# Moving blocks and up weights at other byte offsets in a two-layer encoder kernel

## The chip, the core and the metric

The kernel runs on one core of a Trainium2 chip. The metric is the time on the device in microseconds, taken over repeated runs of the program. The profile is that of one execution, recorded by the hardware profiler. Engines are called as the profile calls them: PE is the matrix engine (TensorE), PEld its weight loads, DVE VectorE, ACT ScalarE, POOL GpSimd, SP SyncE.

## What is computed

Two encoder layers on 256 tokens of width 2048. Each has a token mixer (neighbourhood attention in the first layer, grouped-query attention in the second), run together with cross-attention into 256 memory tokens and one output projection, and then a feed-forward block of width 8192. The change touches the feed-forward block alone:

```python
for i in range(DEPTH):
    ...
    h = h + jnp.concatenate([mix, cross], axis=-1) @ w_o[i]
    n = rms_norm(h, mlp_norm[i])
    h = h + jnp.square(jax.nn.relu(n @ w_up[i])) @ w_down[i]
return rms_norm(h, final_norm)
```

All weights and activations are float32.

## The kernel before

**Two halves for every operand.** TensorE multiplies a shorter float format, so each float32 operand is split into a high and a low part: `split` (L297 to L300) has ScalarE copy the source into the high tile (the write rounds) and VectorE write source minus high into the low tile. A product is then three matmuls: high by high, high by low, low by high.

**The feed-forward block.** The 8192 inner features are cut into 8 parts of 1024. The *up* product of a part (`up_grains`, `u_products`) takes the weights as the stationary operand, 128 by 128 at a time from the tiles `uh` and `ul`, and the activations `hT` as the moving operand, 256 columns. One grain is a half tile of 1024 elements, 24 matmuls; 16 grains make a part, 384 matmuls. `squared` takes the result out, squares it, and makes the stationary tiles `a` of the *down* product.

The down product of the first seven parts (`down_grains`) is one level of Strassen's scheme with seven block products instead of eight. Here the activations `a` are stationary, and the blocks made from the weights are moving, 512 columns at a time: the first group (`FIRST`, three products) from `bh` and `bl` (three blocks each), the second (`SECOND`, four products) from `th` and `tl` (four blocks each). Before the split VectorE and an accumulating transfer on POOL's queue add up the blocks of `t` from those of `b` (L758, L759, L767, L768). One pair of grains is 9 + 12 = 21 matmuls; a part has eight such pairs. The eighth part has no partner and goes through `plain_grains`, with `uh`, `ul`, `th`, `tl` as moving tiles (its matmuls stand at L205, L208 and L209, in the helper `m_products`, which the projections use too, with the moving tiles `hi` and `lo`).

**Order.** `add_mlp` writes the order out by hand: the up grains of part 0 alone, and then, for each of the 56 pairs, up grain, first group, up grain, second group, where the up grains are those of the part after. `run_all` prepares grains some places ahead (`SOON`), so that loads and splits run beside the matmuls. The framework's scheduler then orders the instructions of each engine; in the trace the 48 up matmuls of a pair of grains mostly stand together, followed by the 21 of the pair product. The text calls these 69 a step.

**Where tiles lie.** `bh`, `bl`, `th`, `tl`, `z`, `c` and `a` are in the pool `mlp`, one behind the other from the left of the memory; `bh`, `bl`, `th`, `tl` exist once each. `uh`, `ul` (two buffers each), the loaded weights `U`, `b`, `T` and the scratch tile `junk` are in the pool `side`, which ends at the right. Every tile starts at a multiple of 32 bytes in its partition. `th`, `tl`, `bh`, `bl`, `a`, `hi`, `lo`, `cat` and `memT` start 128 bytes after a multiple of 256; `hT` and `nT`, which share one place, 160 after; `uh`, `ul` and the rest of `side` 224 after. All slices that a matmul reads begin a multiple of 512 bytes into a tile. The memory is nearly full: 1,376 bytes are free between the two sides during the feed-forward block.

**The junk tile.** `sum_squares` (L584) has ScalarE square 512 columns of `h` and keep the sum of each row; the squares themselves go to `junk`, which nothing reads.

Of the kernel before, what the change touches and what calls it, by code (L numbers as in the profile page):

```python
# [11 lines left out]
F32R = mybir.dt.float32r  # L12
BF16 = mybir.dt.bfloat16
# [4 lines left out]
P = 128  # L18
# [15 lines left out]
CH = 2048  # L34
HALF = CH // 2
GROUP = 2
PARTS = 8
PK = DFF // PARTS // P
STEPS = PK // 2
GUARD = 3  # L40
# [30 lines left out]
def encoder_kernel(ctx: ExitStack, tc: tile.TileContext, t: dict, out: bass.AP):  # L71
# [225 lines left out]
    def split(dst_hi, dst_lo, src):  # L297

        nc.scalar.activation(dst_hi, src, AF.Copy)  # L299
        nc.vector.tensor_tensor(dst_lo, src, dst_hi.bitcast(F32), op=ALU.subtract)  # L300
# [281 lines left out]


    def sum_squares(which, i, nb):  # L584
        sq = at.side.tile([P, 512], BF16, tag="junk", bufs=2, name="sq")
        nc.scalar.activation(sq, h[:, i, nb * 512 : (nb + 1) * 512], AF.Square,
                             accum_out=ssq[which][:, i, nb : nb + 1])

# [82 lines left out]
            nc.tensor.matmul(ps, hi[:, s], acts[:, k, SEQ:], start=False, stop=False)  # L671
            nc.tensor.matmul(ps, lo[:, s], acts[:, k, :SEQ], start=False, stop=k == KT - 1)  # L672

    def half_of_side(raw, hf):
        tiles = tuple(at.side.tile([P, HALF], F32R, tag=n, bufs=2, name=n) for n in ("uh", "ul"))
        split(*tiles, raw[:, hf * HALF : (hf + 1) * HALF])
        return tiles

    def loaded(src, tag):
        raw = at.side.tile([P, CH], F32, tag=tag, bufs=2, name=f"raw_{tag}")  # L680
        nc.sync.dma_start(raw, src)
        return raw

    def up_grains(layer, part, m):
        own = {}

        def load():
            own["raw"] = loaded(t[f"w_up{layer}"][part * PK + m], "U")

        def prep(hf):  # L690
            own[hf] = half_of_side(own["raw"], hf)

        def run(hf):
            if hf == 0:
                if part == 0:
                    own["ps"] = at.acc.tile([P, 512], F32, tag="acc", name="ps_u")[:, :SEQ]
                else:
                    if part == 1 and m == 0:
                        closed("ps_acc", "ps_att")
                        at.sums = opened("ps_sums", space=bass.MemoryType.PSUM)  # L700
                        box["ps"] = {}
                    own["ps"] = at.sums.tile([P, 512], F32, tag="up", name="ps_u")[:, :SEQ]
            u_products(own["ps"], hf * (KT // 2), KT // 2, *own.pop(hf))

        def after():
            if part == 0 and m == 0:
                closed("cat", "ring")
                at.mlp = opened("mlp")
                box["z"] = [at.mlp.tile([P, 4, 512], F32, tag=f"z{q}", name=f"z{q}") for q in range(2)]
                box["z_set"] = set()  # L710
            squared(layer, part, m, own["ps"])

        return [Grain(lambda: run(0), None, load, None, lambda: prep(0), SOON),
                Grain(lambda: run(1), after, None, None, lambda: prep(1), SOON)]

    def squared(layer, part, m, ps):
# [8 lines left out]
        if e == 0:  # L725
            return
        if part == PARTS - 1:
            a = at.mlp.tile([P, 2, 4, P], F32R, tag="a", bufs=6, name="a_p")
# [7 lines left out]
        box["a", part, m // 2] = a  # L736
        if part == PARTS - 1 and m == PK - 1 and layer == 1:
            later(2, load_gf)

    def down_grains(layer, part, n, begins, ends):  # L740

        q, j = part % 2 ^ n // STEPS, n % STEPS
        own = {}

        def load():
            src = t[f"w_pair{layer}"][(part * 2 + q) * STEPS + j]
            own["b"] = at.side.tile([P, 3 * 512], F32, tag="b", bufs=2, name="b")
            nc.sync.dma_start(own["b"], src[:, : 3 * 512])
            own["t"] = at.side.tile([P, 4, 512], F32, tag="T", bufs=2, name="t")
            nc.sync.dma_start(own["t"][:, 0, :], src[:, 3 * 512 :])  # L750

        def block(k):

            return own["b"][:, k * 512 : (k + 1) * 512]

        def pre():
            s = own["t"]
            nc.vector.tensor_tensor(s[:, 1, :], s[:, 0, :], block(0), op=ALU.add)  # L758
            nc.gpsimd.dma_start(s[:, 0, :], block(1), accum_op=ALU.add)  # L759

        def prep_first():
            own["first"] = tuple(at.mlp.tile([P, 3 * 512], F32R, tag=x, name=x) for x in ("bh", "bl"))
            split(*own["first"], own["b"])

        def prep_second():
            s = own["t"]
            nc.vector.tensor_tensor(s[:, 2, :], s[:, 1, :], block(1), op=ALU.add)  # L767
            nc.vector.tensor_tensor(s[:, 3, :], s[:, 2, :], block(2), op=ALU.add)  # L768
            own["second"] = tuple(at.mlp.tile([P, CH], F32R, tag=x, name=x) for x in ("th", "tl"))
            split(*own["second"], s.rearrange("p a b -> p (a b)"))  # L770

        def run(which, products):
            hi, lo = own.pop(which)
            a = box["a", part, j]
            for name, ai, bi in products:
                if begins:
                    box["ps"][name] = at.sums.tile([P, 512], F32, tag=name, name=name)
                ps, s = box["ps"][name], slice(bi * 512, (bi + 1) * 512)
                nc.tensor.matmul(ps, a[:, 0, ai, :], hi[:, s], start=begins, stop=False)  # L779
                nc.tensor.matmul(ps, a[:, 0, ai, :], lo[:, s], start=False, stop=False)  # L780
                nc.tensor.matmul(ps, a[:, 1, ai, :], hi[:, s], start=False, stop=ends)  # L781

        def after(products):
            if ends:
                for name, _, _ in products:
                    taken(q, name)

        def after_second():
            after(SECOND)
            if ends:  # L790
                box["z_set"].add(q)
            if ends and (part, n) in FOLDS:
                folded(q)

        return [Grain(lambda: run("first", FIRST), lambda: after(FIRST), load, pre, prep_first, SOON),
                Grain(lambda: run("second", SECOND), after_second, None, None, prep_second, SOON)]

    def columns_of(i, q, b):
# [34 lines left out]
    def plain_grains(layer, nb):  # L833

        last = layer == 1 and nb == 3
        w = Work("M", None, lambda k, i: tuple(box["a", PARTS - 1, k // 2][:, b, k % 2 * 2 + i, :] for b in range(2)),
                 0, True, True, None, finish if last else down_done(layer, nb))
        own = {}

        def load(c):  # L840
            own[c] = loaded(t[f"w_plain{layer}"][nb * 2 + c], "UT"[c])

        def prep(c, hf):
            if c == 0:
                own[c, hf] = half_of_side(own[0], hf)
            else:
                own[c, hf] = tuple(at.mlp.tile([P, CH], F32R, tag=x, name=x) for x in ("th", "tl"))
                split(*own[c, hf], own[1])

        PIECES = ((0, 0, 0, 2), (0, 1, 2, 2), (1, 0, 4, 4))  # L850

        def begin():
            if nb == 0:
                closed("ps_sums")
                open_sums()
            w.ps = [at.acc.tile([P, 512], F32, tag="acc", name="ps_m") for _ in range(NT)]

        def run(n):
            if last:
                return  # L860
            c, hf, k0, nk = PIECES[n]
            if n == 0:
                begin()
            for i in range(NT):
                m_products(w, k0, nk, i, *own[c, hf], n == 0, n == 2)

        def after():
            if not last:
                w.done(w)
                return  # L870

            begin()
            for i in range(NT):
                for n, (c, hf, k0, nk) in enumerate(PIECES):
                    m_products(w, k0, nk, i, *own[c, hf], n == 0, n == 2, keep_order=True)
                w.done(w, i)

        return [Grain(lambda: run(0), None, lambda: load(0), None, lambda: prep(0, 0), SOON),
                Grain(lambda: run(1), None, None, None, lambda: prep(0, 1), SOON),
                Grain(lambda: run(2), after, lambda: load(1), None, lambda: prep(1, 0), SOON)]  # L880

    SOON = (8, 5, 4)
    STEPS_OF = [(p, n) for p in range(PARTS - 1) for n in range(2 * STEPS)]
    HALF_OF = [p % 2 ^ n // STEPS for p, n in STEPS_OF]
    FOLDS = {STEPS_OF[max(i for i, x in enumerate(HALF_OF) if x == q)] for q in range(2)}

    def add_mlp(layer):
        for m in range(PK):
            plan.extend(up_grains(layer, 0, m))
# [309 lines left out]
```

## Time and profile before

| | |
|---|---|
| median of the runs | 2069.38 us (2069.24 to 2069.51, two runs) |
| the profiled execution | 2069.22 us |
| its span, first to last instruction | 2067.2 us |
| granted clock of TensorE, mean | 0.997 |
| PE busy | 2039.7 us, 99% |
| PEld busy | 1815.0 us, 88% |
| DVE busy | 1668.6 us, 81% |
| ACT busy | 1251.3 us, 61% |
| POOL busy | 119.2 us, 6% |
| feed-forward block, first layer | about 445 to 1090 us from the start |
| feed-forward block, second layer | about 1383 to 2060 us |

A row of the profile's groups gives the line, engine and operation, what is written and read, shapes and count, then the busy time of the group in us and the mean length of one instruction in ns, and last the idle time before them with what ended it. A row of the timeline gives the start in us from the start of the span, the length in us, and the instruction; "x4" stands for four of a kind merged. Matmuls overlap in the pipeline, so their lengths add up to more than the time they take: how fast they go is read from the distance of their starts. A row of a window gives its bounds and length, the busy time of PE, PEld, DVE, ACT and POOL with instruction counts, the granted clock, and the share and rate of the DMA engines.

### The profile page before, as it was taken

Reading aid. Unit: us, or ns where it says so; the run is one execution under the profiler, and the core shown is the slowest. Engines: PE = TensorE matmul, PEld = TensorE weight load, DVE = VectorE, ACT = ScalarE, POOL = GpSimd, SP = SyncE. Lnnn points to the kernel's source line nnn. Section 1 sums busy time; section 2 is a strip of 40 time slices with the busy share of each in tenths; the row PEclk is TensorE's granted clock in tenths of the full one; section 3 lists DMA queues with packets and bytes.
Section 4 is the critical chain, followed back from the end, with each engine's and each line's share of the span. In section 5 each row is a group of like instructions: output and inputs, shape, how many; then the busy total and the mean of one; then the engine's idle time right before and its main releaser. Section 6 shows DMA issues by size and latency. Waiting matters only on the chain.

```text
span 2067.2 us, 31544 instructions
## 1 busy us (share of the span) xinstructions
PE 2039.7 (99%) x12516; PEld 1815.0 (88%) x12516; DVE 1668.6 (81%) x2047; ACT 1251.3 (61%) x1642; POOL 119.2 (6%) x144
## 2 busy tenths in 40 slices
PE   8999999999999999999999999999999999999998
PEld 6888888889999999999988888889999999999996
DVE  6767667566899999999996667666988999999896
ACT  6755555555666666666656557555666666666653
POOL 0000000000010000010000001000000000000000
PEclk9999999999999999999999999999999999999999
DMA  7755555736777787787765454536877787777773
GB/s 266 297 183 177 189 175 170 274 105 202 223 235 231 218 240 225 225 240 226 231 201 209 171 177 143 188 138 197 232 227 227 224 242 222 233 232 223 232 225 121
DMA packets 92996, 433.78 MB, mean 210 GB/s; under 512 B 10416, under 2 KB 12080, under 8 KB 59568
## 3 DMA queue, kind: packets, MB, share of 16 engines
q1 hardware_dynamic: 75456, 399.25, 57.3%
q0 software_dynamic: 16816, 31.46, 8.6%
q8 instruction: 98, 1.61, 0.3%
q10 hardware_dynamic: 576, 1.05, 0.1%
q14 instruction: 50, 0.41, 0.1%
HBM read 398.17 MB, written 4.19 MB: 195 GB/s over the span
## 4 chain that ended last, share of the span: by engine, by line
PE 97%; DVE 1%; issue 1%; DMA 1%; ACT 0%; SPq 0%; POOLq 0%; POOL 0%; DVEq 0%; ACTq 0%
PE ps_u L672 11%; PE ps_u L670 11%; PE ps_u L671 11%; PE p L779 9%; PE p L780 9%; PE p L781 9%; PE ps_m L205 8%; PE ps_m L208 8%; PE ps_m L209 8%; PE ps_s L218 7%; PE ps_s L221 3%; PE pt_a L379 1%; PE pt_n L317 0%; PE av L387 0%; PE sc_ps L353 0%
## 5 line engine op out<-in xcount | busy, mean ns | idle before, releaser
L671 PE MATMUL ps_u<-hT,uh 128*128 128x256 f32 x2048 | 569.3, 278 | 3.7 <-DVE hT L325 3.6
L670 PE MATMUL ps_u<-hT,uh 128*128 128x256 f32 x2048 | 569.9, 278 | 1.5 <-ACT uh L299 1.5
L672 PE MATMUL ps_u<-hT,ul 128*128 128x256 f32 x2048 | 569.3, 278 | 1.5 <-DVE ul L300 1.3
L299 ACT ACTIVATE uh<-raw_U 128x1024 fp32r<-128x1024 f32 x278 | 295.0, 1062 | 325.2 <-PE ps_u L671 301.9
L300 DVE TENSOR_TENSOR lo<-raw,hi 128x1024 fp32r<-128x1024 f32 (+1 forms) x222 | 266.3, 1204 | 167.7 <-ACT hi L299 166.4
L671 PEld LDWEIGHTS ps_u<-hT,uh 128*128 128x128 f32 x2048 | 385.9, 188 | 9.1 <-DVE hT L325 4.5
L670 PEld LDWEIGHTS ps_u<-hT,uh 128*128 128x128 f32 x2048 | 386.3, 189 | 7.6 <-ACT uh L299 1.9
L672 PEld LDWEIGHTS ps_u<-hT,ul 128*128 128x128 f32 x2048 | 387.1, 189 | 3.0 <-DVE ul L300 2.3
L300 DVE TENSOR_TENSOR ul<-raw_U,uh 128x1024 fp32r<-128x1024 f32 x278 | 337.9, 1219 | 35.4 <-ACT uh L299 35.4
L299 ACT ACTIVATE hi<-raw 128x1024 fp32r<-128x1024 f32 (+1 forms) x222 | 231.3, 1047 | 218.7 <-PE ps_m L209 116.1
L299 ACT ACTIVATE th<-t 128x2048 fp32r<-128x2048 f32 x112 | 215.2, 1921 | 124.9 <-PE p L781 118.2
L300 DVE TENSOR_TENSOR tl<-t,th 128x2048 fp32r<-128x2048 f32 x112 | 256.3, 2288 | 40.3 <-ACT th L299 39.9
L300 DVE TENSOR_TENSOR bl<-b,bh 128x1536 fp32r<-128x1536 f32 x112 | 196.1, 1751 | 0.4
L780 PE MATMUL p<-tl,a_s 128*128 128x512 f32 x448 | 177.2, 396 | 0.0
L781 PE MATMUL p<-th,a_s 128*128 128x512 f32 x448 | 174.4, 389 | 0.0
L299 ACT ACTIVATE bh<-b 128x1536 fp32r<-128x1536 f32 x112 | 166.2, 1484 | 6.4
L779 PE MATMUL p<-th,a_s 128*128 128x512 f32 x448 | 166.1, 395 | 0.0
L759 POOL DMA_DIRECT2D t<-b x112 | 97.0, 866 | 1168.3 <-DVE t L758 377.5
L218 PE MATMUL ps_s<-nT,hi 128*128 128x512 f32 x448 | 141.7, 394 | 0.0
L781 PE MATMUL p<-bh,a_s 128*128 128x512 f32 x336 | 131.1, 390 | 0.0
L780 PE MATMUL p<-bl,a_s 128*128 128x512 f32 x336 | 130.9, 390 | 0.0
L758 DVE TENSOR_TENSOR t<-t,b 128x512 f32<-128x512 f32 x112 | 77.2, 690 | 48.2 <-DMA t<-in_w_pair 36.4
(235 smaller groups left out, 3510.6 us busy)
## 6 DMA issues: line engine op xcount, KB each, us to landing
raw_U<-in_w_up SPq DMA_DIRECT2D x128, 1024.0 KB, 6.6
b<-in_w_pair SPq DMA_DIRECT2D x112, 768.0 KB, 4.5
raw<-in_w_o SPq DMA_DIRECT2D x32, 1024.0 KB, 5.0
t<-in_w_pair SPq DMA_DIRECT2D x112, 256.0 KB, 3.4
t<-b POOLq DMA_DIRECT2D x112, 256.0 KB, 6.6
raw<-in_w_b SPq DMA_DIRECT2D x21, 1024.0 KB, 5.0
raw<-in_w_av SPq DMA_DIRECT2D x12, 1024.0 KB, 4.9
raw<-in_w_aq SPq DMA_DIRECT2D x12, 1024.0 KB, 4.9
```

The costliest lines, as they stand in the source:

```text
L205: first = nc.tensor.matmul(w.ps[i], ah, hi[:, s], start=st, stop=False)
L208: nc.tensor.matmul(w.ps[i], ah, lo[:, s], start=False, stop=False)
L209: nc.tensor.matmul(w.ps[i], al, hi[:, s], start=False, stop=sp)
L218: nc.tensor.matmul(ps, hi[:, s], acts[:, k0 + j, :], start=k0 + j == 0, stop=False)
L299: nc.scalar.activation(dst_hi, src, AF.Copy)
L300: nc.vector.tensor_tensor(dst_lo, src, dst_hi.bitcast(F32), op=ALU.subtract)
L670: nc.tensor.matmul(ps, hi[:, s], acts[:, k, :SEQ], start=k == 0, stop=False)
L671: nc.tensor.matmul(ps, hi[:, s], acts[:, k, SEQ:], start=False, stop=False)
L672: nc.tensor.matmul(ps, lo[:, s], acts[:, k, :SEQ], start=False, stop=k == KT - 1)
L779: nc.tensor.matmul(ps, a[:, 0, ai, :], hi[:, s], start=begins, stop=False)
L780: nc.tensor.matmul(ps, a[:, 0, ai, :], lo[:, s], start=False, stop=False)
L781: nc.tensor.matmul(ps, a[:, 1, ai, :], hi[:, s], start=False, stop=ends)
```

## The change

The tiles `uh`, `ul`, `bh`, `bl`, `th` and `tl` become 64 elements (256 bytes) wider in each partition, and what is split and multiplied is a stretch of the old width that begins some bytes into the tile. The offset hangs on the layer and the part: `BLOCKS_AT` for the moving blocks of the seven pair parts, `UP_AT` for the up weights of the eight parts, in bytes. The eighth part's down product keeps offset 0, and so do three early weight chunks of the second layer's projections, which borrow `uh` and `ul`. In `moved` the argument in bytes is divided by 4, the size of an element. The junk tile exists once instead of twice.

```diff
+BLOCKS_AT = (0, 4, 8, 16, 24, 32, 40), (48, 56, 252, 248, 240, 160, 144)
+UP_AT = (0, 32, 64, 96, 128, 160, 192, 0), (224, 16, 48, 8, 240, 80, 112, 0)
...
     def sum_squares(which, i, nb):
-        sq = at.side.tile([P, 512], BF16, tag="junk", bufs=2, name="sq")
+        sq = at.side.tile([P, 512], BF16, tag="junk", bufs=1, name="sq")
...
-    def half_of_side(raw, hf):
-        tiles = tuple(at.side.tile([P, HALF], F32R, tag=n, bufs=2, name=n) for n in ("uh", "ul"))
+    def moved(pool, tag, bufs, n, at):
+        return pool.tile([P, n + 64], F32R, tag=tag, bufs=bufs, name=tag)[:, at // 4 : at // 4 + n]
+
+    def half_of_side(raw, hf, at_=0):
+        tiles = tuple(moved(at.side, n, 2, HALF, at_) for n in ("uh", "ul"))
         split(*tiles, raw[:, hf * HALF : (hf + 1) * HALF])
         return tiles
...
         def prep(hf):
-            own[hf] = half_of_side(own["raw"], hf)
+            own[hf] = half_of_side(own["raw"], hf, UP_AT[layer][part])
...
         def prep_first():
-            own["first"] = tuple(at.mlp.tile([P, 3 * 512], F32R, tag=x, name=x) for x in ("bh", "bl"))
+            own["first"] = tuple(moved(at.mlp, x, 1, 3 * 512, BLOCKS_AT[layer][part]) for x in ("bh", "bl"))
             split(*own["first"], own["b"])
...
-            own["second"] = tuple(at.mlp.tile([P, CH], F32R, tag=x, name=x) for x in ("th", "tl"))
+            own["second"] = tuple(moved(at.mlp, x, 1, CH, BLOCKS_AT[layer][part]) for x in ("th", "tl"))
             split(*own["second"], s.rearrange("p a b -> p (a b)"))
...
-                own[c, hf] = tuple(at.mlp.tile([P, CH], F32R, tag=x, name=x) for x in ("th", "tl"))
+                own[c, hf] = tuple(moved(at.mlp, x, 1, CH, 0) for x in ("th", "tl"))
                 split(*own[c, hf], own[1])
```

## The prediction

> **What bounds the kernel now.** I read the page's head and its chain first, then one part of the feed-forward stage by windows, then start times of matmuls in the timeline.
>
> ```profile
> span 2067.2 us, 31544 instructions
> PE 97%; DVE 1%; issue 1%; DMA 1%; ACT 0%; SPq 0%; POOLq 0%; POOL 0%; DVEq 0%; ACTq 0%
> L671 PE MATMUL ps_u<-hT,uh 128*128 128x256 f32 x2048 | 569.3, 278 | 3.7 <-DVE hT L325 3.6
> L780 PE MATMUL p<-tl,a_s 128*128 128x512 f32 x448 | 177.2, 396 | 0.0
> L780 PE MATMUL p<-bl,a_s 128*128 128x512 f32 x336 | 130.9, 390 | 0.0
> 541.00:623.40 82.40, 82.40 (x555) 75.38 (x554) 74.67 (x80) 54.57 (x57) 6.97 (x8) 1.00 0.78 232
> ```
>
> The chain is 97% TensorE. In the stretch of eight steps (its columns: length, PE, PEld, DVE, ACT, POOL, clock, DMA) TensorE is busy without a gap at full clock; VectorE has 82.40 - 74.67 = 7.7 us to spare, ScalarE 28 us. So in these stages the time is the number of matmuls times the distance between their starts, and only that distance matters. The 278 and 396 ns above are lengths with the pipeline in them, not distances. The distances stand in the timeline:
>
> ```profile
> 693.42 0.28 PE L670 MATMUL ps_u<-hT,uh 128*128 128x256 f32 x1
> 698.89 0.40 PE L779 MATMUL p<-th,a_s 128*128 128x512 f32 x1
> 702.13 0.39 PE L779 MATMUL p<-bh,a_s 128*128 128x512 f32 x1
> 703.49 0.39 PE L781 MATMUL p<-bh,a_s 128*128 128x512 f32 x1
> 703.72 0.28 PE L670 MATMUL ps_u<-hT,uh 128*128 128x256 f32 x1
> 704.66 0.28 PE L672 MATMUL ps_u<-hT,ul 128*128 128x256 f32 x1
> 708.74 0.28 PE L672 MATMUL ps_u<-hT,ul 128*128 128x256 f32 x1
> ```
>
> One step is 703.72 - 693.42 = 10.30 us: 48 up matmuls in 698.89 - 693.42 = 5.47, then 21 of the pair product in 703.72 - 698.89 = 4.83. At its best an up matmul takes (708.74 - 704.66) / 36 = 113.3 ns and a pair one (703.49 - 702.13) / 6 = 226.7. At best all the way the step would be 48 x 113.3 + 21 x 226.7 = 10.20, so 0.10 us is lost, all of it just after each turn from one kind to the other.
>
> **Does a place in a tile touch the distance?** Every start is now a multiple of 32 bytes, but not all are alike. The program before puts th, tl, bh, bl, the a tiles, hi, lo, cat and memT 128 bytes past a multiple of 256, hT and nT 160 past one, uh and ul 224. So moving and stationary operand agree modulo 64 in some pairs and differ by 32 in others:
>
> ```profile
> 400.40 0.39 PE L209 MATMUL ps_m<-hi,cat 128*128 128x512 f32 x1
> 403.80 0.39 PE L209 MATMUL ps_m<-hi,cat 128*128 128x512 f32 x1
> 1082.56 0.39 PE L208 MATMUL ps_m<-tl,a_p 128*128 128x512 f32 x1
> 1085.96 0.39 PE L209 MATMUL ps_m<-th,a_p 128*128 128x512 f32 x1
> 1155.20 0.40 PE L208 MATMUL ps_m<-lo,nT 128*128 128x512 f32 x1
> 1157.54 0.40 PE L209 MATMUL ps_m<-hi,nT 128*128 128x512 f32 x1
> 1077.92 0.40 PE L205 MATMUL ps_m<-uh,a_p 128*128 128x512 f32 x1
> 1080.49 0.39 PE L209 MATMUL ps_m<-uh,a_p 128*128 128x512 f32 x1
> 714.63 0.28 PE L672 MATMUL ps_u<-hT,ul 128*128 128x256 f32 x1
> 719.58 0.28 PE L672 MATMUL ps_u<-hT,ul 128*128 128x256 f32 x1
> ```
>
> Moving hi against cat (both 128): 3.40 / 15 = 226.7 ns. th against a_p (both 128): 3.40 / 15 = 226.7. The same hi against nT (128 and 160): 2.34 / 10 = 234.0. uh against a_p (224 and 128): 2.57 / 11 = 233.6. Pairs that agree modulo 64 settle at the short distance; pairs 32 apart stay some 7 ns over it. The last two rows warn: hT against ul agree modulo 64 (160 and 224), and yet this half step ran at 4.95 / 42 = 117.9 ns to its end. So there are two gaits for the same places too, and what came before helps to choose.
>
> [...]
>
> **The change part by part.** Only offsets change; no instruction is added or removed. What counts is the offset modulo 64, because each pair of today agrees modulo 64 at offset 0, and the wider rows (64 elements, 256 bytes) and the missing kilobyte of the junk tile shift every other tile by multiples of 256.
>
> *Pair blocks* (moving; stationary a unmoved), modulo 64: first layer 0, 4, 8, 16, 24, 32, 40; second 48, 56, 60, 56, 48, 32, 16. *Up weights* (stationary; moving hT unmoved): first 0, 32, 0, 32, 0, 32, 0, 0; second 32, 16, 48, 8, 48, 16, 48, 0. Rows show 0 and 32 alone. A difference of 4 or 8 bytes either way (56 and 60 are -8 and -4) I take by the nearest row, as 0; 24 and 40 as 32; 16 and 48 lie as far from both and I take them as 32, since the pace of 32 is what the trace gives wherever a pair doesn't agree. So 8 parts' pair products slow down (first layer parts 3 to 6, second 0 and 4 to 6) and 9 parts' up products (1, 3, 5; 0, 1, 2, 4, 5, 6).
>
> Pair products: 21 x 0.234 = 4.91 in place of 4.83, 0.08 us a step; 8 parts x 8 steps = 64 steps: +5.4 us (unrounded 0.084). Bounds: 0 if no offset matters, 104 steps x 0.084 = +8.7 if all 13 moved parts slow; -104 x 0.07 = -7 if they find the short gait at once (21 x 0.2267 = 4.76).
>
> Up products: 48 x 0.1179 = 5.66 in place of 5.47, 0.187 us a step. Up weights of part p run in the steps of part p - 1, part 0's alone before them. Eight slow parts x 8 steps = 64 x 0.187 = +12.0; part 0 of the second layer, 384 matmuls x 4.6 ns = +1.7. I take 117.9, the one slow row at this width; with the 7 ns that the wide matmuls lose it would be 120.6, 0.32 a step. Bounds: 0, and with all ten parts at 120.6: 72 x 0.32 + 384 x 7.3 ns = +26. Below: -72 x 0.03 = -2.
>
> All of it lies on the chain, as TensorE has no gap there. The covers only grow: VectorE and ScalarE make the same splits, and a longer step gives them more room.
>
> *Splits written and read at other offsets*: taken as unchanged.
>
> ```profile
> L300 DVE TENSOR_TENSOR tl<-t,th 128x2048 fp32r<-128x2048 f32 x112 | 256.3, 2288 | 40.3 <-ACT th L299 39.9
> L300 DVE TENSOR_TENSOR bl<-b,bh 128x1536 fp32r<-128x1536 f32 x112 | 196.1, 1751 | 0.4
> L300 DVE TENSOR_TENSOR ul<-raw_U,uh 128x1024 fp32r<-128x1024 f32 x278 | 337.9, 1219 | 35.4 <-ACT uh L299 35.4
> ```
>
> ul is 32 bytes off the 64-byte grid, tl and bl on it, and all go at the same 1.04 ns an element ((2288 - 1219) / 1024). A part has 8 x (2.288 + 1.751 + 2 x 1.219) = 51.8 us of them and 7.7 us of room: up to 15% more costs nothing.
>
> *The single junk tile*: all its writers are ScalarE's squares, which already follow one another; nothing reads it. 0 us; on the chain only this one stands, with 5.4 us of idle time before it:
>
> ```profile
> 2054.01 0.63 ACT L586 ACTIVATE sq<-h 128x512 bf16<-128x512 f32 x1 [5.44 <-DVE h L935]
> ```
>
> So a wait for the earlier square costs nothing there; in the other places TensorE covers it. *Queues*: the transfers' targets (b, t, raw) keep their offsets modulo 256, and no issue moves.
>
> Sum: 5.4 + 12.0 + 1.7 = 19.1. The profiled execution took 2069.2 (span 2067.2 and 2.0 around it), 0.2 below the median of 2069.38. 2069.2 + 19.1 = 2088.
>
> **The rivals.** *Places don't matter; history does.* The gait is set by what ran before (the 117.9 run speaks for it, the steady pairs against). Then every term is 0: 2069, within 7 either way for gaits that fall otherwise.
>
> *Small offsets break the reading of the moving rows* (the other side). [...] No row has such a start. The nearest is the row at half pace:
>
> ```profile
> 459.20:462.00 2.80, 2.80 (x15) 2.80 (x15) 2.49 (x5) 0.61 (x2) 0.87 (x1) 0.50 0.84 255
> 459.76 0.41 PE L670 MATMUL ps_u<-hT,uh 128*128 128x256 f32 x1
> 460.40 0.41 PE L670 MATMUL ps_u<-hT,uh 128*128 128x256 f32 x1
> ```
>
> At a granted clock of 0.50 the distance is 0.64 / 3 = 213 ns, 100 over 113.3; for 512 columns 200. Two parts (offsets 4 and 252) have 2 x 8 x 21 = 336 such matmuls: +67 us, with the 19 above 2155. Slower by 2% (41.4 us) is reached at (41.4 - 19.1) / 336 = 66 ns each. Against it: 32-byte shifts cost 7 ns, not 100. [...]
>
> *VectorE becomes the bound*: with splits 25% longer at odd offsets a part gains 13 - 7.7 = 5 us, in 13 parts 68: 2137. Nothing in its rows hints at it.
>
> *A better gait*: some offset locks at once everywhere: -7 - 2 = -9, 2060. Over 2% faster would need the distance itself under 113.3 and 226.7, which no row at full clock keeps up.
>
> **How the numbers follow.** The forecast (2076 to 2106) 0.51; places don't matter (2062 to 2076) 0.28; same mechanism, larger (2106 to 2110) 0.05; broken reading 0.11; VectorE 0.02; better gait 0.03. The two largest make the range 2062 to 2106, 8 in 10; its upper end is all bounds together, 8.7 + 26 = 35 over 2069, and a little. The forecast's own range is 2076 to 2106. About 2%, 41 us, is what a measurement of this kernel tells from no change: slower 0.11 + 0.02 = 0.13, faster 0.01, within 0.86.
>
> **What would show it.** By my rule steps (from first up matmul to the next) in the first layer read 10.49, 10.30, 10.49, 10.38, 10.57, 10.38, 10.38 us for parts 0 to 6, in the second 10.57, 10.49, 10.30, 10.49, 10.57, 10.57, 10.38. Slow parts keep near 234 ns (pair) or 118 (up) to the end of a run, where today the distance falls to 226.7 and 113.3. If all steps stay at 10.30, places don't matter. If steps of the parts at 4 and 252 grow by microseconds, the reading breaks. If TensorE gets gaps released by the split of tl or bl, VectorE is the bound. What makes the prediction wrong: 16 and 48 acting like 0, or 4 and 8 like 32, moves it by some 10 us; a price above 10 ns a matmul moves it out of the range.

## The result, and the profile after

| | before | after |
|---|---|---|
| median of the runs, us | 2069.38 (2069.24 to 2069.51) | 2098.25 (2098.15 to 2098.35) |
| span of the profiled execution, us | 2067.2 | 2096.5 |
| granted clock of TensorE, mean | 0.997 | 0.996 |

The changed kernel takes 1.014 times as long (95% interval 1.0096 to 1.0183), 28.9 us more. The forecast was 2088, with a range of 2062 to 2106. The direction held and the time lies in the range, but the rise is half as large again as the 19.1 us of the sum.

First the page of the changed kernel: its head, the chain by engine, and groups (columns as before; the changed kernel's lines stand three to six further down).

```profile
span 2096.5 us, 31546 instructions
PE 97%; DVE 1%; issue 1%; DMA 1%; ACT 0%; SPq 0%; POOLq 0%; POOL 0%; DVEq 0%; ACTq 0%
L674 PE MATMUL ps_u<-hT,uh 128*128 128x256 f32 x2048 | 576.8, 282 | 3.6 <-DVE hT L328 3.6
L303 DVE TENSOR_TENSOR ul<-raw_U,uh 128x1024 fp32r<-128x1024 f32 x278 | 338.2, 1220 | 40.5 <-ACT uh L302 38.9
L303 DVE TENSOR_TENSOR tl<-t,th 128x2048 fp32r<-128x2048 f32 x112 | 256.4, 2289 | 67.3 <-ACT th L302 66.9
L303 DVE TENSOR_TENSOR bl<-b,bh 128x1536 fp32r<-128x1536 f32 x112 | 196.2, 1751 | 0.7 <-ACT bh L302 0.5
L786 PE MATMUL p<-tl,a_s 128*128 128x512 f32 x448 | 177.0, 395 | 0.0
```

The chain is still 97% TensorE, idle time ahead of its groups is as small as before, and the splits go at 1220, 2289 and 1751 ns against 1219, 2288 and 1751. So the loss is neither a wait nor VectorE. The busy lengths hardly show it (576.8 against 569.3 us for one of the three up groups; the pair group even 177.0 against 177.2), because the pipeline's overlap is in them. It stands in the distances between starts. The timeline of the changed kernel, in five steps: the first up matmul (L673), the first of the pair product (L785), and the next step's first up matmul.

```profile
508.20 0.29 PE L673 MATMUL ps_u<-hT,uh 128*128 128x256 f32 x1
513.84 0.39 PE L785 MATMUL p<-th,a_s 128*128 128x512 f32 x1
518.63 0.29 PE L673 MATMUL ps_u<-hT,uh 128*128 128x256 f32 x1
...
591.98 0.28 PE L673 MATMUL ps_u<-hT,uh 128*128 128x256 f32 x1
597.67 0.39 PE L785 MATMUL p<-th,a_s 128*128 128x512 f32 x1
602.65 0.28 PE L673 MATMUL ps_u<-hT,uh 128*128 128x256 f32 x1
...
762.28 0.28 PE L673 MATMUL ps_u<-hT,uh 128*128 128x256 f32 x1
767.93 0.39 PE L785 MATMUL p<-th,a_s 128*128 128x512 f32 x1
...
930.58 0.28 PE L673 MATMUL ps_u<-hT,uh 128*128 128x256 f32 x1
936.33 0.39 PE L785 MATMUL p<-th,a_s 128*128 128x512 f32 x1
941.22 0.28 PE L673 MATMUL ps_u<-hT,uh 128*128 128x256 f32 x1
...
1631.44 0.28 PE L673 MATMUL ps_u<-hT,uh 128*128 128x256 f32 x1
1637.12 0.39 PE L785 MATMUL p<-th,a_s 128*128 128x512 f32 x1
1641.96 0.28 PE L673 MATMUL ps_u<-hT,uh 128*128 128x256 f32 x1
```

Before, each such step was 5.47 + 4.83 = 10.30 us. Part 0 of the first layer (blocks unmoved, up weights of part 1 at 32): 5.64 + 4.79 = 10.43. Part 1 (blocks at 4, up weights at 64): 5.69 + 4.98 = 10.67; here both halves were forecast at the old pace, and both are slow. Part 3 (up weights at 128): the up half takes 5.65 where 5.47 was forecast. Part 5 (up weights at 192): 5.75 + 4.89 = 10.64, the up half again slow against the forecast. Part 2 of the second layer (blocks at 252, up weights at 8): 5.68 + 4.84, the pair half as before and the up half slow.

All 16 up products and 14 pair products, as the mean distance of starts in ns (pauses left out), change times their 384 or 168 matmuls. The text calls a pace that is kept over many matmuls in a row a gait.

| up weights, first layer: at | 0 | 32 | 64 | 96 | 128 | 160 | 192 | 0 |
|---|---|---|---|---|---|---|---|---|
| before, ns | 113.6 | 114.1 | 114.1 | 114.6 | 114.6 | 114.6 | 114.6 | 115.3 |
| after, ns | 113.8 | 117.7 | 118.5 | 119.8 | 117.2 | 117.3 | 119.8 | 115.8 |
| more, us | 0.05 | 1.40 | 1.69 | 2.00 | 1.03 | 1.05 | 2.01 | 0.21 |
| **second layer: at** | 224 | 16 | 48 | 8 | 240 | 80 | 112 | 0 |
| before, ns | 113.6 | 114.1 | 114.1 | 114.6 | 114.6 | 114.6 | 114.6 | 115.3 |
| after, ns | 118.3 | 118.6 | 119.8 | 118.4 | 120.3 | 119.8 | 118.1 | 116.2 |
| more, us | 1.79 | 1.74 | 2.19 | 1.46 | 2.22 | 2.00 | 1.36 | 0.35 |

| pair blocks, first layer: at | 0 | 4 | 8 | 16 | 24 | 32 | 40 |
|---|---|---|---|---|---|---|---|
| after, ns (before 229.6 to 230.0) | 228.2 | 237.3 | 233.2 | 231.3 | 233.5 | 233.1 | 233.5 |
| more, us | -0.31 | 1.28 | 0.61 | 0.28 | 0.65 | 0.58 | 0.59 |
| **second layer: at** | 48 | 56 | 252 | 248 | 240 | 160 | 144 |
| after, ns | 232.6 | 232.2 | 229.4 | 233.4 | 232.9 | 233.9 | 233.0 |
| more, us | 0.44 | 0.43 | -0.04 | 0.63 | 0.55 | 0.71 | 0.51 |

The sums are 22.5 and 6.9 us, together 29.4, and the span grew by 29.3. So the whole change in time lies in the distances of these two kinds of matmul. One of the terms may be chance: the up weights of part 0 of the second layer (224, 1.79 us) also ran at 117.3 to 117.5 ns with offset 0 in the profiles of e3, e8, e10 and e11 below.

### The profile page after: what moved, and what is told of

Same layout as the page of the kernel before. It is cut to its first block, busy times and chain, and to the rows that moved or that the text cites. A ratio compares the mean times of both kernels' runs of the same rounds, so it can differ in the third digit from the quotient of the medians.

```text
span 2096.5 us, 31546 instructions
## 1 busy us (share of the span) xinstructions
PE 2070.4 (99%) x12516; PEld 1839.8 (88%) x12516; DVE 1673.7 (80%) x2047; ACT 1250.6 (60%) x1642; POOL 119.2 (6%) x144
## 3 DMA queue, kind: packets, MB, share of 16 engines
q10 hardware_dynamic: 576, 1.05, 0.1%
## 4 chain that ended last, share of the span: by engine, by line
PE 97%; DVE 1%; issue 1%; DMA 1%; ACT 0%; SPq 0%; POOLq 0%; POOL 0%; DVEq 0%; ACTq 0%
PE ps_u L675 11%; PE ps_u L673 11%; PE ps_u L674 11%; PE p L786 9%; PE p L785 9%; PE p L787 9%; PE ps_m L208 8%; PE ps_m L211 8%; PE ps_m L212 8%; PE ps_s L221 6%; PE ps_s L224 3%; PE pt_a L382 1%; PE pt_n L320 0%; PE av L390 0%; PE sc_ps L356 0%
## 5 line engine op out<-in xcount | busy, mean ns | idle before, releaser
L674 PE MATMUL ps_u<-hT,uh 128*128 128x256 f32 x2048 | 576.8, 282 | 3.6 <-DVE hT L328 3.6
L673 PE MATMUL ps_u<-hT,uh 128*128 128x256 f32 x2048 | 577.4, 282 | 1.5 <-ACT uh L302 1.5
L675 PE MATMUL ps_u<-hT,ul 128*128 128x256 f32 x2048 | 577.3, 282 | 0.8 <-DVE ul L303 0.6
L673 PEld LDWEIGHTS ps_u<-hT,uh 128*128 128x128 f32 x2048 | 388.0, 189 | 8.1 <-ACT uh L302 1.9
L303 DVE TENSOR_TENSOR ul<-raw_U,uh 128x1024 fp32r<-128x1024 f32 x278 | 338.2, 1220 | 40.5 <-ACT uh L302 38.9
L302 ACT ACTIVATE hi<-raw 128x1024 fp32r<-128x1024 f32 (+1 forms) x222 | 231.5, 1047 | 218.7 <-PE ps_m L212 117.9
L303 DVE TENSOR_TENSOR tl<-t,th 128x2048 fp32r<-128x2048 f32 x112 | 256.4, 2289 | 67.3 <-ACT th L302 66.9
L302 ACT ACTIVATE th<-t 128x2048 fp32r<-128x2048 f32 x112 | 215.0, 1919 | 127.0 <-PE p L787 118.5
L303 DVE TENSOR_TENSOR bl<-b,bh 128x1536 fp32r<-128x1536 f32 x112 | 196.2, 1751 | 0.7 <-ACT bh L302 0.5
L786 PE MATMUL p<-tl,a_s 128*128 128x512 f32 x448 | 177.0, 395 | 0.0
L785 PE MATMUL p<-th,a_s 128*128 128x512 f32 x448 | 165.7, 395 | 0.0
L787 PE MATMUL p<-bh,a_s 128*128 128x512 f32 x336 | 132.4, 394 | 0.0
L785 PE MATMUL p<-bh,a_s 128*128 128x512 f32 x336 | 109.9, 395 | 0.0
```

The costliest lines, as they stand in the source:

```text
L673: nc.tensor.matmul(ps, hi[:, s], acts[:, k, :SEQ], start=k == 0, stop=False)
```

## The experiments

Times are ratios to the kernel before, run on the same chip beside each group (its median there 2071.05, 2070.13 and 2071.11 us for the first four, the next four and the last four), with the 95% interval.

| kernel | median, us | ratio | interval |
|---|---|---|---|
| e1, all offsets 0 | 2069.95 | 0.9994 | 0.9984 to 1.0003 |
| e2, up weights moved alone | 2085.91 | 1.0071 | 1.0056 to 1.0086 |
| e3, blocks moved alone | 2080.28 | 1.0044 | 1.0029 to 1.0059 |
| e4, other tiles moved 32 | 2077.06 | 1.0033 | 1.0020 to 1.0045 |
| e5, up weights 128 and 64 | 2081.11 | 1.0056 | 1.0040 to 1.0072 |
| e6, blocks and a both 40 | 2080.26 | 1.0052 | 1.0036 to 1.0068 |
| e7, ring alone moved 32 | 2066.52 | 0.9985 | 0.9975 to 0.9994 |
| e8, e7 and the mlp group moved 64 | 2082.10 | 1.0062 | 1.0044 to 1.0080 |
| e9, blocks 64 and 128 | 2068.33 | 0.9989 | 0.9980 to 0.9998 |
| e10, blocks and a both 16, 8 | 2084.89 | 1.0065 | 1.0051 to 1.0079 |
| e11, a alone 40, 16 | 2090.10 | 1.0091 | 1.0077 to 1.0105 |
| e12, e7 and up weights 128 | 2064.81 | 0.9969 | 0.9959 to 0.9980 |

**e1: the widths without the offsets.** The changed kernel, all offsets 0.

```diff
-BLOCKS_AT = (0, 4, 8, 16, 24, 32, 40), (48, 56, 252, 248, 240, 160, 144)
-UP_AT = (0, 32, 64, 96, 128, 160, 192, 0), (224, 16, 48, 8, 240, 80, 112, 0)
+BLOCKS_AT = (0,) * 7, (0,) * 7
+UP_AT = (0,) * 8, (0,) * 8
```

> All offsets 0; the tiles stay 256 bytes wider and the junk tile single. If only the offsets cost time (agreement modulo 64, history, or a period of 256 bytes): 2069 us within 3, steps of 10.30 us. If the wider rows or the shifted neighbours cost something, part of the 29 us stays and steps are longer than 10.30 with no offset at all.

The time is that of the kernel before, and the steps are 10.30 us again. Wider rows, the shift of the other tiles by multiples of 256 bytes and the single junk tile cost nothing measurable; the offsets make the whole loss.

**e2 and e3: one kind of operand at a time.** e2 keeps the up weights' offsets with the blocks at 0, e3 the reverse.

```diff
 e2
+BLOCKS_AT = (0,) * 7, (0,) * 7
 e3
+UP_AT = (0,) * 8, (0,) * 8
```

> Only the up weights keep their offsets; blocks at 0. Agreement modulo 64: up parts with offsets 64, 128, 192 fall back to 113.3 ns (5.47 us a step), the nine parts that differ stay at 117 to 120 ns; 2081 to 2084 us. Period of 256: parts at 64, 128, 192 stay slow too, 117 to 120 ns; 2087 to 2090. History (the moved blocks before them made the up runs slow): all up runs fast, 2069.

> Only the moving blocks keep their offsets; up weights at 0. Agreement modulo 64, or a period of 256: up runs back at 5.47 us a step, pair products some 7 us in all slower; 2074 to 2078 us. History: up runs behind moved blocks stay at 117 to 120 ns though their own offset is 0, 12 steps parts x 8 x 0.2 us more; 2090 to 2096.

Both medians, 2085.91 and 2080.28 us, lie between the times that their expectations gave for one rule or the other. Together 1.0071 and 1.0044 give 1.0115, less than the 1.014 of both at once but inside its interval (1.0096 to 1.0183). Part 3 of the first layer in e2 shows that the two do not simply add; its timeline:

```profile
759.73 0.28 PE L673 MATMUL ps_u<-hT,uh 128*128 128x256 f32 x1
765.18 0.40 PE L785 MATMUL p<-th,a_s 128*128 128x512 f32 x1
770.01 0.28 PE L673 MATMUL ps_u<-hT,uh 128*128 128x256 f32 x1
```

These up matmuls read weights at 128, as in the step at 762.28 above, with the same places for both operands. There the half took 5.65 us, here 765.18 - 759.73 = 5.45. What differs is the pair product ahead of them: blocks at 16 there, at 0 here. The up weights at 64 keep 118.7 ns in e2 also, and those at 192 keep 119.6. Two steps of e3 follow each other, up weights at 0 in both, blocks at 4:

```profile
600.91 0.28 PE L673 MATMUL ps_u<-hT,uh 128*128 128x256 f32 x1
606.56 0.40 PE L785 MATMUL p<-th,a_s 128*128 128x512 f32 x1
611.56 0.28 PE L673 MATMUL ps_u<-hT,uh 128*128 128x256 f32 x1
617.02 0.40 PE L785 MATMUL p<-th,a_s 128*128 128x512 f32 x1
```

Same tiles, same offsets, same instructions: 5.65 us, then 5.46. An up product at an undisturbed place may take either gait, and takes it for all 48 matmuls. Moved blocks so cost something that the place of the up weights does not explain.

The trace of before has this too, with every tile at one place. All 96 runs of 48 up matmuls stand behind 21 of the pair product and take 114.0 ns; all 14 runs of 46 or 24 that stand behind six of them take 117.7, while the two runs of 24 behind nine take 114.2. The half step of the prediction is one of the 14; here are the first and the last of the six, and its own first matmul:

```profile
712.90 0.39 PE L780 MATMUL p<-bl,a_s 128*128 128x512 f32 x1
714.05 0.39 PE L781 MATMUL p<-bh,a_s 128*128 128x512 f32 x1
714.28 0.28 PE L672 MATMUL ps_u<-hT,ul 128*128 128x256 f32 x1
```

So what TensorE ran just before goes with the gait. But only some places have two gaits: in the changed kernel and in e2 no step whose up weights lie at another place than 0 or 128 went under 116.6 ns.

**e4: make the 32-byte pairs agree.** The kernel before with 32 bytes of padding ahead of the left tiles, so that hi, lo, cat, memT, bh to tl and a begin at 160 instead of 128, like nT; uh and ul stay at 224.

```diff
+    opened("pad").tile([P, 8], F32, name="pad")
```

> The kernel before with 32 unused bytes ahead of the tiles hi, lo, cat, memT, a, bh, bl, th, tl, so that these start 160 past a multiple of 256 and agree modulo 64 with hT, nT, uh, ul. Agreement modulo 64, with the loss at turns due to the change of class: steps of 10.20 us in place of 10.30 (-11 us), the second layer's projections at 226.7 in place of 234 ns (-5 us): 2050 to 2060 us. If a turn costs the same whatever the classes: -5 to -7 us, 2062 to 2064. History alone: 2069.

Of its timeline, one step of the first layer, and then hi against nT:

```profile
505.99 0.28 PE L671 MATMUL ps_u<-hT,uh 128*128 128x256 f32 x1
511.64 0.40 PE L780 MATMUL p<-th,a_s 128*128 128x512 f32 x1
516.43 0.28 PE L671 MATMUL ps_u<-hT,uh 128*128 128x256 f32 x1
...
1155.06 0.39 PE L210 MATMUL ps_m<-hi,nT 128*128 128x512 f32 x1
1157.78 0.39 PE L210 MATMUL ps_m<-hi,nT 128*128 128x512 f32 x1
```

Twelve matmuls of hi and nT in 2.72 us are 226.7 ns, where the prediction's rows gave 234.0: the agreement does shorten them. uh against a goes from a mean of 234.0 to 230.5. Yet the kernel is slower, because every up half of a step takes 5.65 us (117.8 ns), and none of its operands has moved. The expected gain was outweighed by the other gait of the up products, which changed with the place of the pair product's tiles. The pair product itself gains 0.04 a step (4.79).

**e7 and e8: the same pad, taken apart.** e7 puts the 32 bytes ahead of the ring of hi and lo only, so that the tiles of the feed-forward block stay. e8 adds 64 bytes ahead of those tiles: blocks and a move together, and up weights not at all.

```diff
 e7
     def open_ring():
         at.ring = opened("ring")
+        at.ring.tile([P, 8], F32, name="pad_r")
 e8, besides
+                at.mlp.tile([P, 16], F32, name="pad_m")
```

> The kernel before with 32 unused bytes ahead of the ring alone, so hi, lo, cat and memT start at 160 like nT, and the feed-forward tiles stay where they were. Difference theory: the second layer's projections against nT go from 233 to 227 or 228 ns, 792 x 5 ns = 4 us less, all else as before: 2064 to 2066 us (on a chip where before takes 2069). History alone: no change.

> As the run with 32 bytes ahead of the ring, and 64 unused bytes ahead of the feed-forward tiles: a and all blocks at 192, their difference unchanged. If only the difference within a matmul matters: the same as that run, 2064 to 2066 us. If the class of the group before chooses the gait, as 32 bytes here sent all up runs into 117.8 ns: up runs or the first pair products change their pace, by up to 10 us either way.

e7 keeps the gain: hi and lo against nT fall from a mean of 233.2 to 228.0 over 777 matmuls, which is 4.0 us, and the steps stay at 10.30. One product pays: with the roles exchanged, nT moving and hi stationary, the mean rises from 230.4 to 233.0 over 440 matmuls, 1.1 us, and nT against lo (256 columns) falls from 118.2 to 116.0 over 445, 1.0 us. So agreement is not symmetric in the two roles. Of e8, one step of the first layer:

```profile
527.40 0.28 PE L671 MATMUL ps_u<-hT,uh 128*128 128x256 f32 x1
533.06 0.39 PE L781 MATMUL p<-th,a_s 128*128 128x512 f32 x1
537.88 0.28 PE L671 MATMUL ps_u<-hT,uh 128*128 128x256 f32 x1
```

The pair half keeps its 4.82 us, as its operands moved together by 64 bytes. The up half, whose operands did not move, goes to 5.66, in every step, and the kernel takes 15.6 us more than e7, more than the 10 that were expected. In e4 and e8 the splits that write the moved tiles run beside the up matmuls and moved too, so these two runs alone do not tell them from the matmuls ahead. The pair of steps in e3 and the 14 runs of before, where no tile changes its place, speak for the matmuls ahead.

**e5: the period for up weights.** Blocks at 0, all up weights of the first layer at 128, of the second at 64.

```diff
+BLOCKS_AT = (0,) * 7, (0,) * 7
+UP_AT = (128,) * 8, (64,) * 8
```

> Blocks at 0; all up weights of the first layer at 128, all of the second at 64. If the up gait repeats every 128 bytes of difference (my reading of parts 2, 4 and 6 in the run with up offsets alone): first layer as with 0, 5.47 us per 48 up matmuls; second layer 118.5 to 120 ns, 5.7 us per 48, some 7 x 8 x 0.24 + 2 = 15 us in all: 2083 to 2087 us. If the agreement modulo 64 of the prediction holds: both layers fast, 2069 to 2071. If 256 is the period: both slow, about 2100.

A step of each layer:

```profile
510.06 0.28 PE L673 MATMUL ps_u<-hT,uh 128*128 128x256 f32 x1
515.51 0.40 PE L785 MATMUL p<-th,a_s 128*128 128x512 f32 x1
...
1449.41 0.28 PE L673 MATMUL ps_u<-hT,uh 128*128 128x256 f32 x1
1455.11 0.39 PE L785 MATMUL p<-th,a_s 128*128 128x512 f32 x1
1459.89 0.28 PE L673 MATMUL ps_u<-hT,uh 128*128 128x256 f32 x1
```

At 128 the half takes 5.45 us, a little under the 5.47 of before; at 64 it takes 5.70. For the up products agreement modulo 64 is not enough; 128 bytes further they are as fast as at 0. That holds for the steps: the 384 up matmuls that run alone at the head of the first layer's block went at 117.6 ns, the slow gait that the same place can also have. The pair product behind a slow up half goes faster, 4.78 against 4.83: it is at its short distance after three matmuls, where before takes eleven. A slow up half so gives back a little, and the time, 2081.11 us, is 2 us under the range expected.

**e9: the period for blocks.** Up weights at 0, blocks at 64 in the first layer, at 128 in the second.

```diff
+BLOCKS_AT = (64,) * 7, (128,) * 7
+UP_AT = (0,) * 8, (0,) * 8
```

> Up weights at 0; all moving blocks of the first layer at 64, all of the second at 128, stationary a unmoved. If the pair products need only agreement modulo 64: both layers at 229.6 ns in the mean, 2069 to 2072 us. If their gait repeats every 128 bytes, as that of the up products does: first layer 232 to 234 ns, 7 x 8 x 21 x 3.5 ns = 4 us more, second layer as before. If every 256 bytes: both layers slower, 2076 to 2080; the run with 40 in both operands, whose a tiles lie 128 apart in turn, could then not be read.

```profile
534.61 0.39 PE L785 MATMUL p<-th,a_s 128*128 128x512 f32 x1
539.41 0.28 PE L673 MATMUL ps_u<-hT,uh 128*128 128x256 f32 x1
...
1460.48 0.39 PE L785 MATMUL p<-th,a_s 128*128 128x512 f32 x1
1465.37 0.28 PE L673 MATMUL ps_u<-hT,uh 128*128 128x256 f32 x1
```

From the first pair matmul to the next step it is 4.80 us at 64 and 4.89 at 128 (means of 228.8 and 232.7 ns, before 229.7). Counted as offsets, the blocks behave the other way round from the up weights: 64 is good and 128 is not.

Counted as the distance between the two operands, they mostly agree. With hT at 160 past a multiple of 256 and uh and ul at 224, the up operands are already 64 apart at offset 0; at 128 they are 64 apart the other way round, at 64 they are 128 apart, and at 192 they lie at the same place. Blocks and a start at the same place at offset 0. So 64 apart allows the fast pace in both kinds (113.4 to 113.9 ns in parts 1 to 6 of e5 and e9, and 228.8) and 128 apart is slow in both (118.7 and 232.7). They part only at distance 0: the up weights at 192 take 119.6 to 119.8 ns, the slow end, and the pair products 229.7, near the fast one.

The two layers together fit none of the three expectations. The time is still about that of before: at 128 the slower pair half (4.89 against 4.83) is nearly paid for by an up half of 5.44 in place of 5.47.

**e6 and e10: both operands moved together.** The kernel before with blocks and a moved by the same number of bytes, 40 in e6; in e10 16 in the first layer and 8 in the second.

```diff
 e6 (e10 with AT[layer] // 4 in place of 10)
+            a = at.mlp.tile([P, 14*P + 32], F32R, tag="a", bufs=6, name="a_s")[:, 10 : 10 + 14 * P].rearrange("p (x y z) -> p x y z", x=2, y=7)
...
+            own["second"] = tuple(at.mlp.tile([P, CH + 32], F32R, tag=x, name=x)[:, 10 : 10 + CH] for x in ("th", "tl"))
```

> The kernel before with the moving blocks and the stationary tiles a both 40 bytes into wider tiles, so that their difference is as before. If the difference sets the pace: pair products as at 0, about 229.6 ns in the mean, 2069 to 2072 us. [...]

> Blocks and a both moved by 16 bytes in the first layer, by 8 in the second. If the difference set the pace: 229.6 ns in both. If a place off a 32-byte grid costs by itself: about 231 to 234 in both, 2076 to 2080 us. [...]

Pair half of a step in e6:

```profile
513.46 0.40 PE L780 MATMUL p<-th,a_s 128*128 128x512 f32 x1
518.37 0.28 PE L670 MATMUL ps_u<-hT,uh 128*128 128x256 f32 x1
```

4.91 us; the means are 233.6 to 234.0 ns in all parts of e6, 231.5 to 232.0 at 16 and 233.3 to 233.6 at 8. But the difference is not 0 throughout. The tiles are 128 bytes wider here, not 256, so that modulo 256 bl and tl begin 128 further than bh and th, and every second buffer of a 128 further than the one before it. In half of the matmuls the operands lie 128 apart, which e9 shows to be slow (232.7 ns). Of the matmuls of bh and th, those whose a does lie at the same place modulo 256 take 233.8 ns at 40, 233.1 at 8 and 230.8 at 16, where before has 229.1. The mixture is the same at all three offsets, so 40 and 8 cost 2 to 3 ns more than 16 by their own place: at these two offsets a difference of 0 does not protect. Whether 16 costs anything by itself these runs do not show. The time of e10, 2084.89 us, is 5 us over what was expected, because the up products, not moved, also slowed, to 115.7 ns in most parts of the first layer and 116.4 in the second.

**e11: the stationary operand alone.** The blocks keep offset 0 and a is moved by 40 in the first layer and 16 in the second. The tiles are as wide as in e6, so here too bl and tl, and every second buffer of a, begin another 128 bytes further.

```diff
+AT = 40, 16
-            a = at.mlp.tile([P, 2, 7, P], F32R, tag="a", bufs=6, name="a_s")
+            a = at.mlp.tile([P, 14*P + 32], F32R, tag="a", bufs=6, name="a_s")[:, AT[layer] // 4 : AT[layer] // 4 + 14 * P].rearrange("p (x y z) -> p x y z", x=2, y=7)
...
+            own["second"] = tuple(at.mlp.tile([P, CH + 32], F32R, tag=x, name=x)[:, : CH] for x in ("th", "tl"))
```

> Only the stationary tiles a moved, by 40 bytes in the first layer and 16 in the second; blocks at 0. If the moving operand's own place were all that counts: 229.6 ns in both, 2069 to 2071 us. If the stationary one's place counts as the rows of hi against nT say: 231 to 234 in both, 2075 to 2080.

```profile
534.99 0.40 PE L781 MATMUL p<-th,a_s 128*128 128x512 f32 x1
539.93 0.29 PE L671 MATMUL ps_u<-hT,uh 128*128 128x256 f32 x1
...
1475.55 0.39 PE L781 MATMUL p<-th,a_s 128*128 128x512 f32 x1
1480.46 0.29 PE L671 MATMUL ps_u<-hT,uh 128*128 128x256 f32 x1
```

4.94 and 4.91 us (means 234.1 at 40, 233.5 at 16, in most parts). Matmuls of bh and th whose a lies just 40 further take 234.5 ns, just 16 further 233.4, where before has 229.1. No run has these wider tiles with a at 0, so the share of the 128 bytes is not known; but e10 has the same tiles with both operands at 16, and there the mean is 231.7. Some 2 of the 4 ns at 16 so come from moving a away from the blocks. The up products behind them, not moved, rise to 116.8 and 115.6 ns in most parts. This was the slowest of the experiments, 10 us over the range expected.

**e12: the good places together.** e7, and uh and ul 128 bytes into wider tiles.

```diff
+        at.ring.tile([P, 8], F32, name="pad_r")
-        tiles = tuple(at.side.tile([P, HALF], F32R, tag=n, bufs=2, name=n) for n in ("uh", "ul"))
+        tiles = tuple(at.side.tile([P, HALF + 64], F32R, tag=n, bufs=2, name=n)[:, 32 : 32 + HALF] for n in ("uh", "ul"))
```

> A version that should beat both kernels: 32 unused bytes ahead of the ring (4 us less in its own run), and the up weights 128 bytes into wider tiles, where the first layer of the run on periods had 43.7 us in place of 44.0 for each part's up matmuls: another 2 to 4 us. Ratio to before 0.996 to 0.998. If the gain of 0.3 us a part was chance: 0.9985, as with the ring alone.

```profile
529.44 0.28 PE L671 MATMUL ps_u<-hT,uh 128*128 128x256 f32 x1
534.88 0.40 PE L780 MATMUL p<-th,a_s 128*128 128x512 f32 x1
539.71 0.28 PE L671 MATMUL ps_u<-hT,uh 128*128 128x256 f32 x1
```

Up half 5.44 and pair half 4.83, 10.27 a step. It is the fastest kernel of the study, 0.9969 of the time before (0.9959 to 0.9980). The 4 us of e7 and 112 steps x 0.03 us = 3.4 make 7.4, and 0.0031 x 2069 = 6.4 were measured, but the traces do not confirm this sum. In the profiled execution, the longest of the eight (2067.65 us), the up matmuls that run alone at the head of both layers' blocks took 117.6 and 117.9 ns in place of 113.6, which costs 3.2 us and takes the gain of the steps back. The interval also touches that of e7 (0.9975 to 0.9994), so what the 128 bytes add is not shown for sure. Blocks at 64 besides were not tried with it.

## Why the prediction was right, and where it fell short

**Right: what bounds the kernel and that the distance between starts carries the change.** The 29.4 us found in the distances are the whole growth of the span. The splits go as fast as before (1220, 2289 and 1751 ns in the mean, and no part stands out), so VectorE did not become the bound, and e1 shows the widths and the junk tile at nothing.

**Right: places matter.** The rival that they do not (0.28) falls: with everything else the same, e1 and the changed kernel differ by the offsets alone. The rival of the broken reading falls too: the blocks at 4 and 252 cost 237.3 and 229.4 ns, +8 and 0, not +200. That price was an estimate from the row at half clock, and no run shows a start that costs as much. The rival of the better gait falls for the whole; only the pair product of part 0, whose blocks did not move, went from 230.0 to 228.2.

**Terms against measured.** The parts forecast slow: up weights 13.7 forecast (12.0 and 1.7), 15.7 measured; pair products 5.4 forecast, 4.3 measured. These two prices were about right, at 117 to 120 ns and 231 to 234. The parts forecast at no cost: up weights 0 forecast, 6.8 measured; pair products 0 forecast, 2.6 measured. 19.1 + 2.0 - 1.1 + 6.8 + 2.6 = 29.4.

**The step that failed** is "What counts is the offset modulo 64", as a rule for all pairs. It took the up weights at 64, 128 and 192 as unchanged. e5 shows that modulo 64 is too coarse for them: 64 is slow (118.7), 128 fast in the steps (113.4 to 113.9 in parts 1 to 6). So 64 and 192 cost 1.69 and 2.01 us, and no row of before has an up matmul at another place, from which it could have been read. e9 shows the same of the blocks: 64 fast (228.8), 128 slow (232.7). By the distance between the operands the two kinds agree better: at 64 both can be fast (113.4 to 113.9 and 228.8), at 128 both are slow (118.7 and 232.7). The operands of before were 64 apart in the up products and 0 in the pair products, and the rule took these two for the same. 8 bytes taken "by the nearest row, as 0" was wrong for both operands (1.46 us for the up weights, 0.61 and 0.63 for blocks at 8 and 248), and so was 4 (1.28); only 252 was as forecast.

**The second gap: history was seen and priced at 0.** The prediction said of its 117.9 run that "what came before helps to choose". The up weights at 128 cost 1.03 us in the changed kernel and nothing in e2 (5.45 us a half step), where the blocks ahead of them lay at 0; e3, e4 and e8 slow up products whose own places are the old ones (5.65, 5.65 and 5.66 us). This is part of the 6.8. The prediction took its one slow half step for a warning; that all 14 runs of before behind six pair matmuls were slow (117.7 ns), and none behind 21 (114.0), could have been counted in that trace.

**Luck.** The time fell into the range although the sum was 10 us short. It was the width of the range, 2076 to 2106 for the forecast alone, that took in the 9.4 us of the parts taken at nothing, and not a term of the working.

**What stays open.** Which part of the chip makes the pace hang on the places of both operands; why operands at the same place are slow in the up products (119.6 to 119.8 ns) and not in the pair products (229.7), and whether the width (512 or 256 columns), the roles of the operands or the neighbours decide that; what it is in the matmuls ahead that chooses the gait; why 4 is the worst place for blocks (237.3) and 252 nearly the best (229.4); why up weights at 240 held 122.9 ns in a few steps, which no other place showed. The rule found is an outline: at offsets that are no multiple of 32 slow throughout the changed kernel but for 252 (up weights 118.1 to 120.3 ns, blocks 231.3 to 237.3), at multiples of 32 with the fast gait open where the operands lie 64 apart (113.4 to 113.9 and 228.8), and otherwise as measured.

## What to carry to other kernels

Where TensorE runs back to back, look at the distance between matmul starts, not at busy lengths: if equal matmuls show two distances some 3 to 4% apart (226.7 and 233, 113.3 and 118 here), the places of the tiles are worth a look, and e7 gained from 32 bytes of padding (0.9985 of the time). When a tile is widened to move what is in it, widen it by a multiple of 256 bytes, as the changed kernel does (e1, with these widths and no offset, took 0.9994 of the time): the 128 bytes of e6, e10 and e11 moved the neighbours as well. Measure each pair of operands, and the group that runs after it too, since a good place for one can put the next in the slow gait, as in e4 (hi against nT from 234.0 to 226.7 ns, the up products to 117.8). A rule read from two sorts of places (0 and 32) does not tell what 64 or 128 do; count places from the other operand's, not from the old one.

## What the runs showed of the hardware beyond that

- A gait lasts: with equal operands, 48 up matmuls run at 113.3 to 114.0 or at 117.7 to 117.8 ns in the mean of their run (e3). In before the 96 runs behind 21 pair matmuls all take the one (114.0) and the 14 behind six all the other (117.7).
- The distance of the two operands counts: 64 bytes apart allows the fast pace (113.4 to 113.9 ns and 228.8) and 128 is slow (118.7 and 232.7) for both kinds of product (e5, e9), and moving both by 64 leaves the pair product at 4.82 us (e8).
- Equal instructions at equal places may go either way from one execution to another. The changed kernel and e1 are alike up to the end of the 384 up matmuls that run alone at the head of the first layer's block; in their profiles these went at 113.8 and 117.4 ns, a difference of 1.4 us, and the runs of one kernel spread by some 5 us (e1: 2067.85 to 2072.63).
- The place of the stationary operand counts, not only that of the moving one: 118.7 ns with the up weights alone at 64 (e5), 114.1 to 114.6 before.
- The losses of one matmul are of like size at both widths: 3 to 6 ns on a mean of 114.1 to 114.6 for 256 columns with the stationary operand moved, 2 to 8 on 229.7 for 512 columns with the moving one moved. That it is the width which does not matter is not shown, as the operand moved differs too.
